# Where the tiles lie in SBUF: rooms laid out in a given order, with gaps of 32 bytes between kinds of tile

## The chip, the cores and the metric

The kernel runs on one core of one Trainium2 chip. The metric is the device time of one execution in microseconds; three runs of the kernel before gave 2304.89 to 2305.59 us, median 2305.21.

## What is computed

Two layers of a decoder trunk over 1024 tokens of width 1024, in float32. Each layer has two head groups side by side (a retention group and a differential attention group), an output projection, and a SwiGLU feed-forward part:

```
def reference(x, attn_norm, w_in, ...):
    h = x
    for l in range(DEPTH):                              # DEPTH = 2
        u = rmsnorm(h, attn_norm[l])
        rq, rk, rv, rg, dq, dk, dv = split(u @ w_in[l])
        ret = silu(rg) * rmsnorm(retention_chunkwise(rq, rk, rv), ret_norm[l])
        dif = rmsnorm(diff_attention(dq, dk, dv, lam), diff_norm[l]) * (1.0 - lam_init)
        h = h + concat([ret, dif]) @ w_out[l]
        u = rmsnorm(h, ffn_norm[l])
        h = h + (silu(u @ w_gate[l]) * (u @ w_up[l])) @ w_down[l]   # hidden size 2816
    return rmsnorm(h, final_norm)
```

## The kernel before

Activations lie feature-major: 128 features on the partitions, tokens along the row. Every large product is made of TensorE matmuls with a 128x128 block of weights as the stationary operand and 512 tokens of an activation as the moving operand. Float32 accuracy comes from splitting each operand into a high part and a low part and adding three matmuls: high weights times high activations, high weights times low activations, low weights times high activations. `mm3` (L270 to L272) does this for the projections, the output projection and the tail of the down projection; `product` (L246 to L248) does it for gate, up and most of the down projection, which go by a Strassen-like scheme of seven products in place of eight. `tm_pair` (L305 to L307) makes token-major values with the roles turned round: the activation `u` is stationary and the weights move, 256 columns at a time.

```
for i, (bh, bl) in enumerate(b):
    c = slice(P * i, P * i + P)
    mm(ps, lhsT=wh[:, c], rhs=bh, ...)       # L246
    mm(ps, lhsT=wh[:, c], rhs=bl, ...)       # L247
    mm(ps, lhsT=wl[:, c], rhs=bh, ...)       # L248
```

Each matmul is an instruction pair: a weight load (LDWEIGHTS, shown as PEld) and the matmul itself (MATMUL, shown as PE). The weight load of the next matmul runs beside the matmul before it.

The names of the tiles are their tags. `w` (12 tiles of 128x512) holds the split weights. The moving operands of the big products are in `u` (4 tiles of 8x512), `ka`, `v` and `sp` (4 tiles of 1024 each); the line `TAGS7 = ["u", "u", "ka", "v", "u", "u", "sp"]` says which tag holds the moving operand of each of the seven products, so four of seven are in `u` and one each in `ka`, `v` and `sp`. Raw weights arrive by DMA in `wr` (some in `kb`), the stream of hidden activations in `mx`; `a4` (shown as `a`) holds the residual stream and attention tiles, `t2` (shown as `t`) is for temporaries, and `acc`, `nx`, `ny`, `z`, `m` are small. PE's order is written out by hand, and in the feed-forward part the order of ScalarE (ACT), VectorE (DVE), GpSimd (POOL) and the DMA queue (SP) too; elsewhere a scheduler orders those four.

A tag gets its room in SBUF (a fixed number of buffers) when it is first asked for, one room behind the other along each partition, in steps of 32 bytes. All big tiles are multiples of 2048 bytes long, and every slice that TensorE reads of the big tiles begins at a multiple of 512 bytes in its tile, so for all the big products the place of an operand modulo 256 is that of its room. The rooms in the built program of before, in bytes modulo 256:

| room | w | u | ka | v | mx | t2 | sp | a4 | wr | kb | acc |
|---|---|---|---|---|---|---|---|---|---|---|---|
| before, modulo 256 | 224 | 224 | 224 | 224 | 224 | 224 | 96 | 96 | 96 | 96 | 96 |
| moving minus `w`, modulo 256 | | 0 | 0 | 0 | | | 128 | | | | |

Of the kernel before, what the change touches and what calls it, by code (L numbers as in the profile page):

```python
# [13 lines left out]
R32 = mybir.dt.float32r  # L14
# [4 lines left out]
P = 128  # L19
D = 1024  # L20
T = 1024
KT = D // P
NH = 2
HT = T // NH
# [5 lines left out]
FAST = 16  # L30
TAILS = [2, 4]
TAGS7 = ["u", "u", "ka", "v", "u", "u", "sp"]
RAWS = ["wr", "wr", "wr", "kb", "kb"]
EPS = 1e-6
NEG = -3.0e38
# [83 lines left out]
class Line:  # L119


    def __init__(self):
        self.n, self.tasks, self.products, self.w, self.made = -1, {}, [], {}, 0
# [23 lines left out]
class Trunk:  # L147
    def __init__(self, tc, ctx, a):
        self.tc, self.nc, self.a = tc, tc.nc, a
        pool = lambda name, **kw: ctx.enter_context(tc.tile_pool(name=name, bufs=1, **kw))  # L150
        self.sb = pool("sb")
        self.ps = pool("ps", space=bass.MemoryType.PSUM)
        self.dr = pool("dr", space=bass.MemoryType.DRAM)
        self.n = 0
        self.wi = 0
        self.consts()


    def t(self, tag, bufs, shape, dt=F32):
# [290 lines left out]
    def seven_second(self, h, gcol, b, keep, line):  # L450
# [10 lines left out]
        b11, b21 = [keep[i // 2][:, c[i % 2]] for i in range(4)], [keep[2 + i // 2][:, c[i % 2]] for i in range(4)]  # L461
        b += [self.views(TAGS7[2]), self.views(TAGS7[3]), None, self.views(TAGS7[5]), None]
        two = [self.big("sp") for _ in range(2)]
# [6 lines left out]
        def sub(out, x, z, q=None, i=0):  # L470
            v(out=out, in0=x, in1=z, op=ALU.subtract)
            if q is not None:
                nc.scalar.copy(b[q][i][0], out)
# [12 lines left out]
        def room(q):  # L486
            b[q] = self.views(TAGS7[q])
        ops += [lambda i=i: sub(b11[i], t22[i], t12[i]) for i in r]
# [561 lines left out]
    def right_factors(self, line, fast, m0):  # L1050
# [14 lines left out]
        def one(q, i):  # L1065
            if not b[q]:
                b[q] += self.views(TAGS7[q])
            self.part(stage[q, i - i % 2][:, 512 * (i % 2):512 * (i % 2) + 512], b[q][i],
# [9 lines left out]
    def down_fast(self, line, h, at, f0, b, m):  # L1078
# [3 lines left out]
        for e in range(2):  # L1082
            self.factors(line, at + 2 * e, {j: n0 + 2 * j + e for j in range(7)}, None,
                         [RAWS[(m + e) % 5], RAWS[(m + 2 + e) % 5]],
                         [n for n in range(n0, n0 + 14) if n % 3 == 0])
# [25 lines left out]
    def layer(self, l, h, us, w_first, norm1, after):  # L1111
# [22 lines left out]
        keep = [self.big("mx") for _ in range(4)]  # L1134
        b = [self.views(tag) for tag in TAGS7[:2]]
        self.two_halves(h, 4, ws, rhs, ["mm"], self.seven_first(h, 16 + 8 * l, b, keep))
# [130 lines left out]
```

## Time and profile before

| what | value |
|---|---|
| median of 3 runs | 2305.21 us (2304.89 to 2305.59) |
| profiled execution, its own time | 2305.69 us |
| its span (first to last instruction) | 2303.9 us |
| granted TensorE clock, mean | 0.995 |
| PE busy | 2262.5 us (98%), 11328 matmuls |
| PEld busy | 1897.3 us (82%), 11328 weight loads |
| DVE, ACT, POOL busy | 1391.0, 1008.9, 762.5 us |
| DMA queue | 28.9% of 16 engines' span |

The profiled execution took 1.8 us more than its span, and is 0.5 us above the median. PE's busy time counts matmuls that are pipelined: a 512-column matmul is shown as some 390 ns long while the next one starts some 230 ns after it, so two stand one over the other and what counts for the time is the distance from start to start. A wait of PE is shown in the columns on idle time and in the list of waits.

### The profile page before, as it was taken

The page shows a single profiled execution, that of the slowest core. Times are in us where ns is not written, and L with a number is a line of the kernel's source. Part 1 is how long each engine was busy: PE and PEld are TensorE (multiplying, and loading weights), DVE is VectorE, ACT ScalarE, POOL GpSimd, SP SyncE. Part 2 cuts the span into 40 slices and gives each one's busy share as a digit, 9 for nine tenths or more (in the row PEclk, how much of TensorE's full clock was granted, in tenths as well). Part 3 has the DMA queues.
Part 4 walks back from the last instruction along what each step waited for, and adds up shares of the span by engine and source line. Part 5 has one row for each costly group of instructions (what it writes and reads, how often), then busy time and mean ns, then how long its engine had stood idle before and what let it go on. Part 6 is the DMA issues. An engine that isn't in the chain of part 4 may idle for free.

```text
span 2303.9 us, 30680 instructions
## 1 busy us (share of the span) xinstructions
PE 2262.5 (98%) x11328; PEld 1897.3 (82%) x11328; DVE 1391.0 (60%) x2576; ACT 1008.9 (44%) x1905; POOL 762.5 (33%) x608
## 2 busy tenths in 40 slices
PE   8999999999999999999999999999999999999998
PEld 5888898887788888888888888988878888888887
DVE  8777603987534333895567775058874434359856
ACT  5666623445333333543257665244443333344332
POOL 3111212122545455336121112211234545544350
PEclk9999999999999999999999999999999999999999
DMA  5212121112332332752232222102123232346422
GB/s 166 75 47 65 46 92 40 53 55 64 123 115 92 114 106 89 232 185 94 73 99 55 56 65 92 55 29 74 55 87 119 89 118 90 110 148 200 157 65 74
DMA packets 74214, 216.58 MB, mean 94 GB/s; under 512 B 8016, under 2 KB 10064, under 8 KB 74064
## 3 DMA queue, kind: packets, MB, share of 16 engines
q1 hardware_dynamic: 74064, 214.62, 28.9%
q8 instruction: 89, 1.46, 0.3%
q14 instruction: 61, 0.50, 0.1%
HBM read 162.16 MB, written 44.04 MB: 90 GB/s over the span
## 4 chain that ended last, share of the span: by engine, by line
PE 82%; DVE 10%; DMA 2%; ACT 2%; issue 2%; POOL 1%; DVEq 0%; SPq 0%; ACTq 0%; POOLq 0%
PE ps_mm L246 7%; PE ps_mm L248 7%; PE ps_mm L247 7%; PE ps_mm L271 7%; PE ps_mm L270 7%; PE ps_mm L272 7%; PE ps_s L247 4%; PE ps_s L246 4%; PE ps_s L248 4%; PE ps_mm L307 3%; PE ps_mm L305 3%; PE ps_mm L306 3%; PE ps_t L246 3%; PE ps_t L248 3%; PE ps_t L247 3%
## 5 line engine op out<-in xcount | busy, mean ns | idle before, releaser
L223 POOL TENSOR_TENSOR w<-wr,w 128x512 fp32r<-128x512 f32 x278 | 390.5, 1418 | 469.4 <-ACT w L222 436.9
L263 POOL TENSOR_TENSOR w<-wr,w 128x512 fp32r<-128x512 f32 x140 | 184.9, 1327 | 577.7 <-ACT w L262 520.5
L270 PE MATMUL ps_mm<-u,w 128*128 128x512 f32 (+1 forms) x735 | 295.9, 403 | 0.0
L271 PE MATMUL ps_mm<-u,w 128*128 128x512 f32 (+1 forms) x735 | 287.1, 391 | 2.0 <-DVE u L432 2.0
L272 PE MATMUL ps_mm<-u,w 128*128 128x512 f32 (+1 forms) x735 | 287.3, 391 | 0.0
L222 ACT CAST w<-wr 128x512 fp32r<-128x512 f32 x312 | 187.8, 619 | 143.7 <-DVE wr L893 88.3
L246 PE MATMUL ps_mm<-u,w 128*128 128x512 f32 x432 | 168.8, 391 | 0.1
L247 PE MATMUL ps_mm<-u,w 128*128 128x512 f32 x432 | 168.4, 390 | 0.0
L248 PE MATMUL ps_mm<-u,w 128*128 128x512 f32 x432 | 168.3, 390 | 0.0
L272 PEld LDWEIGHTS ps_mm<-u,w 128*128 128x128 f32 x735 | 138.0, 188 | 30.2
L271 PEld LDWEIGHTS ps_mm<-u,w 128*128 128x128 f32 x735 | 138.4, 188 | 25.9 <-DVE u L432 2.7
L270 PEld LDWEIGHTS ps_mm<-u,w 128*128 128x128 f32 x735 | 138.3, 188 | 23.8
L942 ACT COPY t<-ps_mm 128x512 f32<-128x512 f32 x76 | 44.6, 586 | 246.3 <-PE ps_mm L248 246.1
L262 ACT CAST w<-wr 128x512 fp32r<-128x512 f32 x140 | 85.7, 619 | 129.1 <-PE ps_mm L271 39.0
L305 PE MATMUL ps_mm<-w,u 128*128 128x256 f32 x448 | 128.6, 287 | 0.0
L307 PE MATMUL ps_mm<-w,u 128*128 128x256 f32 x448 | 127.8, 285 | 0.1
L306 PE MATMUL ps_mm<-w,u 128*128 128x256 f32 x448 | 127.6, 285 | 0.0
L223 POOL TENSOR_TENSOR w<-t,w 128x512 fp32r<-128x512 f32 x52 | 74.7, 1436 | 147.7 <-ACT w L222 147.7
L559 DVE CUSTOM_DVE_ANT_0 sp<-ps_s,wr 128x512 f32<-128x512 f32 (+2 forms) x192 | 102.8, 551 | 33.2 <-PE ps_s L557 32.2
L563 ACT ACTIVATE sp<-sp,m 128x256 f32<-128x256 f32 (+7 forms) x128 | 99.2, 775 | 50.8 <-DVE m L562 50.1
L851 DVE TENSOR_TENSOR a<-a,ps_mm 128x512 f32<-128x512 f32 (+1 forms) x148 | 98.5, 666 | 33.4 <-PE ps_mm L248 19.9
L246 PE MATMUL ps_t<-u,w 128*128 128x512 f32 x288 | 113.2, 393 | 4.8 <-ACT t L942 4.8
(386 smaller groups left out, 5832.7 us busy)
## 6 DMA issues: line engine op xcount, KB each, us to landing
wr<-wts SPq DMA_DIRECT2D x190, 512.0 KB, 3.7
mx<-s_fast SPq DMA_DIRECT2D x56, 512.0 KB, 4.9
s_fast<-mx SPq DMA_DIRECT2D x48, 512.0 KB, 5.0
kb<-ka SPq DMA_DIRECT2D x64, 128.0 KB, 2.3
s_rest<-mx SPq DMA_DIRECT2D x12, 512.0 KB, 2.9
kb<-wts SPq DMA_DIRECT2D x12, 512.0 KB, 6.0
mx<-s_rest SPq DMA_DIRECT2D x12, 512.0 KB, 3.8
a<-xT SPq DMA_DIRECT2D x16, 256.0 KB, 5.4
```

The lines of the kernel that those rows point to most:

```text
L222: nc.scalar.copy(h, src)
L223: (eng or nc.gpsimd).tensor_tensor(out=o, in0=src, in1=h.bitcast(F32), op=ALU.subtract)
L246: mm(ps, lhsT=wh[:, c], rhs=bh, start=first and i == 0, stop=False, skip_group_check=True)
L247: mm(ps, lhsT=wh[:, c], rhs=bl, start=False, stop=False, skip_group_check=True)
L248: mm(ps, lhsT=wl[:, c], rhs=bh, start=False, stop=i == 3, skip_group_check=True)
L263: nc.gpsimd.tensor_tensor(out=o, in0=raw[:, cols], in1=h.bitcast(F32), op=ALU.subtract)
L270: mm(out, lhsT=lh, rhs=rh, start=first, stop=False)
L271: mm(out, lhsT=lh, rhs=rl, start=False, stop=False)
L272: mm(out, lhsT=ll, rhs=rh, start=False, stop=last)
L305: mm(o, lhsT=uh, rhs=wh, start=k == 0, stop=False)
L306: mm(o, lhsT=uh, rhs=wl, start=False, stop=False)
L307: mm(o, lhsT=ul, rhs=wh, start=False, stop=k == KT - 1)
```

## The change

`rooms()` runs ahead of everything else and asks once for one tile of certain tags, in the order of a list; this fixes where their rooms lie. A number in the list puts a gap of that many bytes. The other tags follow by first use, as before. Nothing else differs: on every engine the instructions, their order, their shapes and their waits are the same as before, and only the addresses are others.

```
+ROOMS = ["w", 32, "ka", 32, "v", 32, "sp", "nx", "ny", "u"]
...
+        self.rooms()
         self.consts()
+
+    def rooms(self):
+
+        for i, x in enumerate(ROOMS):
+            if isinstance(x, int):
+                self.const(f"gap_{i}", [P, x // 4])
+            elif x == "u":
+                self.t("u", 4, [P, KT, HT], R32)
+            elif x in ("w", "t2", "acc"):
+                self.t(x, {"w": 12, "t2": 5, "acc": 2}[x], [P, 512])
+            elif x in ("nx", "ny"):
+                self.t(x, 2, [P, 4])
+            elif x in ("z", "m"):
+                self.t(x, 4, [P, 4])
+            else:
+                self.big(x)
```

`nx` and `ny` take 128 bytes between them, so `u` comes 128 behind `sp`. The rooms in the built program of the changed kernel:

| room | w | u | ka | v | mx | t2 | sp | a4 | wr | kb | acc |
|---|---|---|---|---|---|---|---|---|---|---|---|
| after, modulo 256 | 128 | 96 | 160 | 192 | 64 | 64 | 224 | 64 | 64 | 64 | 64 |
| moving minus `w`, modulo 256 | | 224 | 32 | 64 | | | 96 | | | | |

## The prediction

> **What bounds the kernel now.** I read the page's first two parts, then the list of PE's waits, then PE's groups by form, and last the timeline of single matmuls.
>
> ```profile
> span 2303.9 us, 30680 instructions
> ...
> PE 2262.5 (98%) x11328; PEld 1897.3 (82%) x11328; DVE 1391.0 (60%) x2576; ACT 1008.9 (44%) x1905; POOL 762.5 (33%) x608
> ...
> PEclk9999999999999999999999999999999999999999
> ...
> PE 82%; DVE 10%; DMA 2%; ACT 2%; issue 2%; POOL 1%; DVEq 0%; SPq 0%; ACTq 0%; POOLq 0%
> ```
>
> PE is busy in 98% of the span, at nearly full clock in every slice, and 82% of the chain that ended last is PE. The list of PE's waits says the same from the other side; these are its two longest:
>
> ```profile
> PE ps_mm L289 <- DMA a<-xT: 5.2, 1, 5.2
> PE ps_t L246 <- ACT t L942: 4.8, 2, 2.4
> ```
>
> So the time is the sum of the distances from one matmul's start to the next, and the other engines follow. An edit that only moves addresses counts where it changes that distance.
>
> **Does an address change it? The trace of before holds two cases.** The moving tiles `u`, `ka`, `v` lie 0 bytes off the weights `w` modulo 256, `sp` 128 bytes off. The groups by form (busy us, mean ns of one):
>
> ```profile
> L270 PE MATMUL ps_mm<-u,w 128*128 128x512 f32 x729 | 294.3, 404 | 0.0
> L272 PE MATMUL ps_mm<-u,w 128*128 128x512 f32 x729 | 285.6, 392 | 0.0
> L271 PE MATMUL ps_mm<-u,w 128*128 128x512 f32 x729 | 285.4, 392 | 2.0 <-DVE u L432 2.0
> L246 PE MATMUL ps_mm<-u,w 128*128 128x512 f32 x432 | 168.8, 391 | 0.1
> L247 PE MATMUL ps_mm<-u,w 128*128 128x512 f32 x432 | 168.4, 390 | 0.0
> L248 PE MATMUL ps_mm<-u,w 128*128 128x512 f32 x432 | 168.3, 390 | 0.0
> ...
> L247 PE MATMUL ps_t<-u,w 128*128 128x512 f32 x288 | 112.6, 391 | 0.0
> ...
> L247 PE MATMUL ps_s<-u,w 128*128 128x512 f32 x224 | 87.2, 389 | 0.0
> ...
> L246 PE MATMUL ps_mm<-sp,w 128*128 128x512 f32 x216 | 85.7, 397 | 2.8 <-DVE t L954 2.8
> L248 PE MATMUL ps_mm<-sp,w 128*128 128x512 f32 x216 | 85.3, 395 | 0.0
> L247 PE MATMUL ps_mm<-sp,w 128*128 128x512 f32 x216 | 85.1, 394 | 0.0
> ...
> L247 PE MATMUL ps_mm<-ka,w 128*128 128x512 f32 x216 | 84.1, 389 | 0.0
> ...
> L247 PE MATMUL ps_s<-v,w 128*128 128x512 f32 x192 | 74.7, 389 | 0.0
> ```
>
> Same instruction, same shape, same lines: 389 to 391 ns where moving tile and weights lie 0 apart, (397 + 395 + 394) / 3 = 395.3 ns where they lie 128 apart. A shown duration contains the next matmul's start, so I check it on the timeline (start us, length us), where twelve `sp` matmuls are followed by `u`:
>
> ```profile
> 560.65 0.40 PE L246 MATMUL ps_mm<-sp,w 128*128 128x512 f32 x1
> 560.89 0.39 PE L247 MATMUL ps_mm<-sp,w 128*128 128x512 f32 x1
> ...
> 563.44 0.39 PE L246 MATMUL ps_mm<-u,w 128*128 128x512 f32 x1
> 563.68 0.40 PE L247 MATMUL ps_mm<-u,w 128*128 128x512 f32 x1
> 563.91 0.39 PE L248 MATMUL ps_mm<-u,w 128*128 128x512 f32 x1
> 564.14 0.39 PE L246 MATMUL ps_mm<-u,w 128*128 128x512 f32 x1
> ...
> 564.59 0.39 PE L248 MATMUL ps_mm<-u,w 128*128 128x512 f32 x1
> ...
> 566.18 0.39 PE L246 MATMUL ps_t<-u,w 128*128 128x512 f32 x1
> ```
>
> Twelve `sp` matmuls take 563.44 - 560.65 = 2.79 us, 232.5 ns from start to start. The first three `u` matmuls behind them still take 233 ns each (564.14 - 563.44 = 0.70 us); the last seven before 566.18 take 1.59 us, 227 ns each. Two things follow. The difference of 5 ns in the durations is one of start-to-start distance. And at 0 bytes the short distance is a state that PE settles into: for the first matmuls behind a disturbance the same operands cost what 128 bytes cost.
>
> By the Trainium skill none of this should be. The page "TensorE: Matmul & The Clock Gate", section "Step-by-step: what each phase is for", says that loading the next tile's weights takes no SBUF read bandwidth from the running matmul, since the two have ports of their own. By that rule the change is worth nothing and the sum stays at 2305. The rows of `sp` against those of `u` speak against it; its rival is weighed below.
>
> **The change, part by part.** The order, the shapes and the waits of all instructions stay, so each term is a count of matmuls by a change of distance. The new residues are 224 (that is, 32 below) for `u`, 32 for `ka`, 64 for `v`, 96 for `sp`. No row of before shows any of these, so each is bounded by the rows at 0 and at 128 and, below, by the shortest matmul of any of these tiles (minimum / median / maximum ns):
>
> ```profile
> L247 PE MATMUL ps_mm<-u,w x432: 387/389/398, 504.0 to 2210.3; 128*128 128x512 f32 x144
> ...
> L247 PE MATMUL ps_mm<-ka,w x216: 387/389/397, 539.3 to 2199.4; 128*128 128x512 f32 x108
> ...
> L247 PE MATMUL ps_mm<-sp,w x216: 387/393/399, 560.9 to 2221.3; 128*128 128x512 f32 x108
> ```
>
> None of the three goes below 387 ns in any phase, and at 0 bytes the median of 389 is already within 2 ns of it. So there is little to win at `u`, `ka`, `v` (1 to 3 ns each) and 6 ns to lose.
>
> - `u` in gate, up and down (L246 to L248): 3 x (432 + 288 + 224) = 2832 matmuls, now 390 ns. At the price of `sp`: 2832 x 5.3 = +15.0 us; at the median of 389: -2.8.
> - `u` in the projections (L270 to L272): 3 x 729 = 2187, now 392 (L270's 404 holds the waits at a group's start; I price it as the other two). 2187 x 3.3 = +7.2; or 2187 x -3 = -6.6.
> - `ka`: 648 matmuls at 389: 648 x 6.3 = +4.1, or 0. `v`: 576 at 389: +3.6, or 0.
> - `sp`, 648 matmuls, 128 to 96: I take 0, since 128 is the nearest row; -4.1 if it comes down to 389.
>
> Which end for `u` and `ka`? By distance, 32 bytes are nearer to 0 than to 128. I still take the end of 128 for all three, because the timeline shows that the long distance is what PE runs at whenever it is out of the settled state, with 0 bytes too: the long one looks like the general case, the short one like a coincidence of two streams that must meet exactly. It is a choice with little behind it, hence its modest chance. For `v` at 64, halfway, the same choice has more behind it.
>
> - `tm_pair` (weights moving, `u` stationary, 256 columns) goes from 0 to 32. Its rows, and one of 128 bytes:
>
> ```profile
> L305 PE MATMUL ps_mm<-w,u 128*128 128x256 f32 x448 | 128.6, 287 | 0.0
> L306 PE MATMUL ps_mm<-w,u 128*128 128x256 f32 x448 | 127.6, 285 | 0.0
> ...
> L601 PE MATMUL ps_o<-a,v 128*128 128x256 f32 x160 | 40.0, 285 | 0.0
> ```
>
> At 256 columns 0 and 128 bytes cost the same within 2 ns, so I take 0; the ends are 1344 x -2 = -2.7 and 1344 x 5.3 = +7.1.
>
> - ACT and POOL read and write the same rooms. Their rows (POOL's with two inputs) at 128 bytes (`wr` or `kb` with `w`) and at 0 (`t` with `w`, `mx` with `u`):
>
> ```profile
> L223 POOL TENSOR_TENSOR w<-wr,w 128x512 fp32r<-128x512 f32 x278 | 390.5, 1418 | 469.4 <-ACT w L222 436.9 <-issue 15.0 <-PE ps_s L248 8.6
> ...
> L223 POOL TENSOR_TENSOR w<-t,w 128x512 fp32r<-128x512 f32 x52 | 74.7, 1436 | 147.7 <-ACT w L222 147.7
> L223 POOL TENSOR_TENSOR w<-kb,w 128x512 fp32r<-128x512 f32 x28 | 40.9, 1462 | 76.9 <-ACT w L222 76.9
> L238 POOL TENSOR_TENSOR u<-mx,u 128x512 fp32r<-128x512 f32 x14 | 20.4, 1463 | 8.5 <-ACT u L237 7.6 <-PE ps_mm L271 0.4 <-PE ps_mm L272 0.4
> ```
>
> 1418 and 1462 at 128, 1436 and 1463 at 0: no order by address. I take 0. Were there a few per cent, POOL's idle time in the first row (469.4 us beside 390.5 busy) and PE's short waits above cover it. The gap tiles and the first request of each tag issue nothing.
>
> Sum: 15.0 + 7.2 + 4.1 + 3.6 = +29.9 us on the profiled execution's 2305.7 us (span 2303.9 and 1.8 around it): 2335.6; the median of before is 0.5 lower, so 2335. Both ends: all at the low ones gives -2.8 - 6.6 - 4.1 - 2.7 = -16, thus 2289; all high with `tm_pair` gives +37, thus 2342, and a residue worse than 128 would go beyond.
>
> **Rivals.**
> 1. Nothing happens (2305). Either the two ports never meet, and `sp` is slow for another reason (it ends each set of seven products, and its users wait on DVE's sums), or the settled state is wide enough to take 32 and 64 bytes. For it: medians of 389 at three different tiles, and the distance argument. Against: twelve `sp` matmuls in a row at 232.5 ns with no wait between them. It decides if `u` keeps a median of 389.
> 2. Faster (2293). PE settles at 224 as at 0, or sooner behind each disturbance, and `sp` at 96 comes into reach: -4.1 for `sp`, -6.6 for the projections' `u`, -2.8 for the other `u`, less what `ka` and `v` may give back; I take -12. The place is L270 to L272: 392 ns against 389 is what the way into the settled state costs today. It decides if `sp` falls under 391 while `u` does not rise.
> 3. Only the tiles 64 and more off lose (2309): `v` +3.6, `tm_pair` a little, `u` and `ka` unchanged.
>
> A further sentence of the skill points at more: the same page's "Back-to-back issue gap" gives N / 2.4 + 2.5 ns, thus an estimate of 216 ns at 512 columns, 11 ns under the settled 227. By that page some 6200 matmuls would gain up to 68 us if addresses alone stood between. The minimum of 387, at 0 and at 128 alike, shows no such matmul.
>
> **How the numbers follow.** Forecast (`u` at the price of 128, with most or all of the others): 0.46. Rival 1: 0.21. Rival 2: 0.25. Rival 3: 0.08, half of it within 0.2%. Changes of 0.2% (4.6 us) are about what a measurement of this kernel can tell from none. So faster 0.25, same 0.25, slower 0.50. The range of 8 in 10 must reach both sides: down to 2291, which leaves out only the best of rival 2, and up to 2345, a little over the high ends. Within the forecast alone it is 2322 to 2347, since `u` may be dearer or cheaper at 224 than `sp` at 128.
>
> **What would show it.** In the changed kernel's groups by form, `u` of L246 to L248 at 394 to 397 shows the forecast right, 389 to 390 shows it wrong, whatever the others do. `ka`, `v` and `sp` are three more readings of the same curve, at 32, 64 and 96. L305 to L307 outside 283 to 289 would upset the zero for `tm_pair`. PE's idle time should stay as small as it is; if it grows, or if POOL's 1418 moves by more than 50 ns, another engine feels the addresses and the argument from PE alone fails. What would make it wrong is mainly the choice of the end for 224: 5019 of the 6243 matmuls priced hang on that one residue.

## Result: 1.1% slower, and the profile after

The changed kernel takes 2330.22 us (median of 4 runs, 2329.69 to 2331.28) beside 2305.1 us for the kernel before on the same chip: a ratio of 1.0108 (95% interval 1.0093 to 1.0123). The profiled execution took 2329.69 us, its span 2327.9 us, at the same granted clock of 0.995. In the changed kernel's file the numbers of the lines are 18 higher: the product is L264 to L266, the projections L288 to L290, `tm_pair` L323 to L325.

The page of the changed kernel, its busy times and the shares of the chain that ended last:

```profile
span 2327.9 us, 30680 instructions
...
PE 2291.4 (98%) x11328; PEld 1895.1 (81%) x11328; DVE 1386.7 (60%) x2576; ACT 1010.4 (43%) x1905; POOL 758.4 (33%) x608
...
PE 86%; DVE 9%; ACT 2%; issue 1%; DMA 0%; POOL 0%; DVEq 0%; ACTq 0%; POOLq 0%
```

PE alone is busier, by 2291.4 - 2262.5 = 28.9 us; ACT, DVE, POOL and the weight loads stay within 4.5 us. PE's idle time (span less busy) went from 41.4 to 36.5 us, so 4.9 of the 28.9 us did not reach the end. The list of PE's waits has the same two at its top as before:

```profile
PE ps_mm L307 <- DMA a<-xT: 5.5, 1, 5.5
PE ps_t L264 <- ACT t L960: 4.7, 2, 2.4
```

The groups by form (busy us, mean ns of one) show where the 28.9 us are:

```profile
L288 PE MATMUL ps_mm<-u,w 128*128 128x512 f32 x729 | 296.9, 407 | 0.0
L289 PE MATMUL ps_mm<-u,w 128*128 128x512 f32 x729 | 288.2, 395 | 1.8 <-DVE u L450 1.8
L290 PE MATMUL ps_mm<-u,w 128*128 128x512 f32 x729 | 287.6, 395 | 0.0
L266 PE MATMUL ps_mm<-u,w 128*128 128x512 f32 x432 | 171.1, 396 | 0.0
...
L323 PE MATMUL ps_mm<-w,u 128*128 128x256 f32 x448 | 127.2, 284 | 0.0
L324 PE MATMUL ps_mm<-w,u 128*128 128x256 f32 x448 | 126.2, 282 | 0.2 <-POOL w L281 0.2
L325 PE MATMUL ps_mm<-w,u 128*128 128x256 f32 x448 | 126.0, 281 | 0.0
...
L265 PE MATMUL ps_t<-u,w 128*128 128x512 f32 x288 | 115.3, 400 | 0.0
...
L265 PE MATMUL ps_s<-u,w 128*128 128x512 f32 x224 | 88.6, 396 | 0.0
...
L266 PE MATMUL ps_mm<-sp,w 128*128 128x512 f32 x216 | 85.2, 394 | 0.0
L265 PE MATMUL ps_mm<-ka,w 128*128 128x512 f32 x216 | 85.1, 394 | 0.0
L266 PE MATMUL ps_s<-v,w 128*128 128x512 f32 x192 | 75.6, 394 | 0.0
L265 PE MATMUL ps_s<-v,w 128*128 128x512 f32 x192 | 75.3, 392 | 0.0
L264 PE MATMUL ps_s<-v,w 128*128 128x512 f32 x192 | 74.9, 390 | 0.0
```

The reader is to see that every group with `u`, `ka` or `v` moving grew, most by 3 to 7 ns per matmul, `v` by 1 to 5 (the 400 of `ps_t` holds a stretch at half speed that is shown further below), `sp` hardly at all, and `tm_pair`, with 256 columns and the roles turned round, became 3 to 4 ns cheaper. The timeline shows that it is again the distance from start to start, as in the quoted stretch of before:

```profile
564.92 0.39 PE L264 MATMUL ps_mm<-u,w 128*128 128x512 f32 x1
...
567.01 0.40 PE L264 MATMUL ps_mm<-u,w 128*128 128x512 f32 x1
```

Nine `u` matmuls in 2.09 us, 232 ns each, where the last seven of before took 227 ns each. Further on in such rows `u` goes on at 231.7 and 234.8 ns in turn: the settled state that it had at 0 bytes is gone.

### The profile page after: what moved, and what is told of

Same layout as the page of the kernel before. It is cut to its first block, busy times and chain, and to the rows that moved or that the text cites. A ratio compares the mean times of both kernels' runs of the same rounds, so it can differ in the third digit from the quotient of the medians.

```text
span 2327.9 us, 30680 instructions
## 1 busy us (share of the span) xinstructions
PE 2291.4 (98%) x11328; PEld 1895.1 (81%) x11328; DVE 1386.7 (60%) x2576; ACT 1010.4 (43%) x1905; POOL 758.4 (33%) x608
## 4 chain that ended last, share of the span: by engine, by line
PE 86%; DVE 9%; ACT 2%; issue 1%; DMA 0%; POOL 0%; DVEq 0%; ACTq 0%; POOLq 0%
PE ps_mm L264 8%; PE ps_mm L265 8%; PE ps_mm L266 8%; PE ps_mm L289 7%; PE ps_mm L288 7%; PE ps_mm L290 7%; PE ps_s L266 4%; PE ps_s L265 4%; PE ps_s L264 4%; PE ps_t L264 3%; PE ps_t L265 3%; PE ps_t L266 3%; PE ps_mm L325 2%; PE ps_mm L323 2%; PE ps_mm L324 2%; PE ps_s L574 1%
## 5 line engine op out<-in xcount | busy, mean ns | idle before, releaser
L288 PE MATMUL ps_mm<-u,w 128*128 128x512 f32 (+1 forms) x735 | 298.6, 406 | 0.0
L290 PE MATMUL ps_mm<-u,w 128*128 128x512 f32 (+1 forms) x735 | 289.3, 394 | 0.0
L266 PE MATMUL ps_mm<-u,w 128*128 128x512 f32 x432 | 171.1, 396 | 0.0
L265 PE MATMUL ps_mm<-u,w 128*128 128x512 f32 x432 | 170.9, 396 | 0.0
L264 PE MATMUL ps_mm<-u,w 128*128 128x512 f32 x432 | 170.9, 396 | 0.0
L290 PEld LDWEIGHTS ps_mm<-u,w 128*128 128x128 f32 x735 | 138.1, 188 | 32.9
L288 PEld LDWEIGHTS ps_mm<-u,w 128*128 128x128 f32 x735 | 138.3, 188 | 25.8
L323 PE MATMUL ps_mm<-w,u 128*128 128x256 f32 x448 | 127.2, 284 | 0.0
L325 PE MATMUL ps_mm<-w,u 128*128 128x256 f32 x448 | 126.0, 281 | 0.0
L264 PE MATMUL ps_t<-u,w 128*128 128x512 f32 x288 | 115.4, 401 | 4.7 <-ACT t L960 4.7
```

The lines of the kernel that those rows point to most:

```text
L264: mm(ps, lhsT=wh[:, c], rhs=bh, start=first and i == 0, stop=False, skip_group_check=True)
L265: mm(ps, lhsT=wh[:, c], rhs=bl, start=False, stop=False, skip_group_check=True)
L266: mm(ps, lhsT=wl[:, c], rhs=bh, start=False, stop=i == 3, skip_group_check=True)
L288: mm(out, lhsT=lh, rhs=rh, start=first, stop=False)
L290: mm(out, lhsT=ll, rhs=rh, start=False, stop=last)
L323: mm(o, lhsT=uh, rhs=wh, start=k == 0, stop=False)
```

## The experiments

All start from the changed kernel and alter the list ROOMS (three of them also give one tag two rooms), so one row of residues (moving tile less weights, modulo 256) describes each. The theory: what a matmul of 512 columns costs hangs on where its moving tile lies against the weights modulo 256, whatever the tile, the line or the place in the program. The rivals are named with the runs.

**All tiles at 0.** `sp` too goes to the weights' residue.

```
-ROOMS = ["w", 32, "ka", 32, "v", 32, "sp", "nx", "ny", "u"]
+ROOMS = ["w", "ka", "v", "sp", "u", "mx", "t2", "a4", "wr", "kb", "acc"]
```

> All big rooms (w, ka, v, sp, u, mx, t2, a4, wr, kb, acc) lie at one residue modulo 256, so every moving tile is 0 bytes off its weights. Theory 1 (what counts is moving minus weights, modulo 256, and 0 is the cheap one): sp falls from 395 to 389-390 ns (648 x 6 = -3.9 us), the mixed pairs of before (u with kb, ka with a, some 400 matmuls) fall by about 5 (-2 us), u, ka, v stay at 389-391; time about 2299. Theory 2 (sp is slow since it ends each set of seven products and its users wait): sp stays at 395, time 2305. Theory 3 (a tile's own place modulo 256 counts, whatever the weights' place): all tiles have moved to another residue than before, so u, ka and v move away from 389 as well.

Measured: 2299.61 us, ratio to before 0.9972 (0.9961 to 0.9983). Groups by form:

```profile
L266 PE MATMUL ps_mm<-u,w 128*128 128x512 f32 x432 | 168.1, 389 | 0.0
...
L323 PE MATMUL ps_mm<-w,u 128*128 128x256 f32 x448 | 128.1, 286 | 0.0
...
L265 PE MATMUL ps_mm<-sp,w 128*128 128x512 f32 x216 | 84.1, 389 | 0.0
```

`sp` falls from 394 to 389 ns, the value of all others. So `sp` was dear for its address and not for its place in the program. From start to start, against weights in `w` and with distances over 300 ns left out, the mean falls by 5.8 ns for `sp` (4.5 us over its 770 matmuls) and by 0.3 ns for `u` (1.6 us over its 5138), though `u` lies at 0 in both; the reason for the second is in the section on why the prediction was right. Against the few weights that lie in `kb`, 128 off in before, the same `u` falls from 232.8 to 226.7 ns.

**The residues crossed over:** `sp` at 0 (256 modulo 512), and `u`, `ka`, `v` at 128.

```
+ROOMS = ["w", "z", "u", "ka", "v", "mx", "t2", "nx", "ny", "sp", "a4", "wr", "kb", "acc"]
```

> The rooms of w alone are put 128 bytes further against all other rooms of before: u, ka, v become 128 off w, sp becomes 0 off (256 modulo 512); the other rooms keep their distances among one another. Theory 1: a cross-over, u, ka, v go to 394-396 and sp falls to 389-390; 2832 x 5.3 + 2187 x 3.3 + 4.1 + 3.6 - 4.1 = +26, about 2331. Theory 2: sp stays at 395 and u at 390, 2305. Theory 3: only w changed its relation, so moving tiles keep their order (sp slower than u). If the period were 512 and not 256, sp would not fall to 389 although u rises.

Measured: 2328.52 us, ratio 1.0101 (1.0086 to 1.0116).

```profile
L266 PE MATMUL ps_mm<-u,w 128*128 128x512 f32 x432 | 170.6, 395 | 0.0
...
L266 PE MATMUL ps_mm<-ka,w 128*128 128x512 f32 x216 | 85.3, 395 | 0.0
...
L265 PE MATMUL ps_mm<-sp,w 128*128 128x512 f32 x216 | 84.3, 390 | 0.0
...
L266 PE MATMUL ps_s<-v,w 128*128 128x512 f32 x192 | 75.8, 395 | 0.0
```

The tiles change prices: what was 389 is 395, and `sp` at 256 bytes costs 390. The price follows the address, and it repeats with 256 bytes.

**`u` alone moved, to 224; the rest as before.**

```
+ROOMS = ["w", "ka", "v", "mx", "t2", "z", "sp", "a4", "wr", "kb", "acc", "nx", 32, "u"]
```

> Only u is put where the change puts it (224 off w); ka, v, mx, t2 stay 0 off and sp, a, wr, kb, acc 128 off as before. Theory 1: u at 395-396, ka and v 389, sp 395; tm_pair (w minus u is 32) 281-284 as in the changed kernel. 2832 x 5.5 + 2187 x 3.3 - 1344 x 3 = +19, about 2324, most of the change's +25. Theory 3b (the small rooms or the neighbours' order matter, not u's distance): 2305.

Measured: 2323.0 us, ratio 1.0075 (1.006 to 1.009), thus +17 us of the change's +25.

```profile
L265 PE MATMUL ps_mm<-u,w 128*128 128x512 f32 x432 | 170.9, 396 | 0.0
...
L324 PE MATMUL ps_mm<-w,u 128*128 128x256 f32 x448 | 125.9, 281 | 0.0
...
L264 PE MATMUL ps_mm<-ka,w 128*128 128x512 f32 x216 | 84.7, 392 | 0.0
...
L266 PE MATMUL ps_mm<-ka,w 128*128 128x512 f32 x216 | 84.0, 389 | 0.0
...
L266 PE MATMUL ps_s<-v,w 128*128 128x512 f32 x192 | 74.7, 389 | 0.0
```

The tile that moved changed, and with it `tm_pair`, which has the same `u` as its stationary operand. `ka` at 0 is 3 ns dearer in its first two lines, since it now follows a `u` at another residue.

**`u` left at 0, the others moved** (`ka` 32, `v` 64, `sp` 96).

```
+ROOMS = ["w", "u", "mx", "t2", 32, "ka", 32, "v", 32, "sp", 32, "a4", "wr", "kb", "acc"]
```

> The other half of the change: ka 32, v 64, sp 96 off w, u back at 0. Theory 1: u 389-391, ka 395, v 390-394, sp 394-398 as in the changed kernel, tm_pair back at 285-287: 648 x 6 + 576 x 3 + 648 x 1 = +6, about 2311. e3 and e4 together should add up to the change's +25. If they do not, the parts act on one another.

Measured: 2313.0 us, ratio 1.0033 (1.002 to 1.0045), thus +7 us. The two halves add up: 17 + 7 = 24 beside 25 for the whole.

```profile
L266 PE MATMUL ps_mm<-u,w 128*128 128x512 f32 x432 | 168.1, 389 | 0.0
...
L324 PE MATMUL ps_mm<-w,u 128*128 128x256 f32 x448 | 127.6, 285 | 0.0
...
L266 PE MATMUL ps_mm<-ka,w 128*128 128x512 f32 x216 | 85.4, 396 | 0.0
```

**Other residues for each tile:** `u` 64, `v` 160, `sp` 192, `ka` 224.

```
+ROOMS = ["w", "mx", "t2", "nx", "u", "ny", "a4", "wr", "kb", "acc", 32, "v", 32, "sp", 32, "ka"]
```

> The same kinds of distance, given to other tiles: u 64 off w, ka 224, v 160, sp 192. Theory 1 (the distance sets the price, whichever tile it is): u takes what v had at 64 in the changed kernel (L264 390, L265 392, L266 394, in place of 389-390 at 0), ka takes what u had at 224 (395-396), and v and sp give two new readings at 160 and 192, expected with the long ones at 394-397; 5019 x 3 + 648 x 6 + 576 x 6 + 0 = +22, about 2327. Theory 3 (the tile's place in the chain of products sets it): v stays at 390-394, u at 395-396, 2330. 64 would then be the only distance besides 0 that is partly cheap.

Measured: 2314.53 us, ratio 1.0038 (1.0024 to 1.0052). The time expected was 2327: a miss by 12 us.

```profile
L290 PE MATMUL ps_mm<-u,w 128*128 128x512 f32 x729 | 286.8, 393 | 0.0
L266 PE MATMUL ps_mm<-u,w 128*128 128x512 f32 x432 | 170.4, 394 | 0.0
...
L264 PE MATMUL ps_mm<-u,w 128*128 128x512 f32 x432 | 169.4, 392 | 0.0
L323 PE MATMUL ps_mm<-w,u 128*128 128x256 f32 x448 | 126.1, 281 | 0.0
...
L324 PE MATMUL ps_mm<-w,u 128*128 128x256 f32 x448 | 125.0, 279 | 0.0
...
L265 PE MATMUL ps_mm<-sp,w 128*128 128x512 f32 x216 | 85.2, 395 | 0.0
```

Two reasons: `u` at 64 costs 392 to 394 ns and in the projections only 1 ns more than before, and `tm_pair`, whose weights now lie 192 from `u`, takes 279 to 281 ns in place of 285 to 287, some 8 us over 1344 matmuls. The expectation had priced the second at nothing.

**Whose weights: the matmul's own, or those loaded beside it?** The high and the low part of the weights get rooms of their own. In the control both lie at 0:

```
-        h, o = self.t("w", 12, [P, 512], R32), self.t("w", 12, [P, 512], R32)
+        h, o = self.t("wh", 6, [P, 512], R32), self.t("wl", 6, [P, 512], R32)
...
+ROOMS = ["wh", "wl", "ka", "v", "sp", "u", "mx", "t2", "a4", "wr", "kb", "acc"]
```

> Control for the next run: all rooms at one residue as in e1, but the high and the low weights in rooms of their own (6 tiles each, handed out in the same turn). Every theory: as e1, about 2300, with 389-391 ns in L264, L265 and L266 alike.

Measured: 2299.2 us, ratio 0.9974 (0.9963 to 0.9986), like all tiles at 0. Splitting the room alone does nothing. Then the low part 128 off:

```
+ROOMS = ["wh", "ka", "v", "sp", "u", "mx", "t2", "a4", "wr", "kb", "acc", "z", "wl"]
```

> As e6, but the room of the low weights lies 128 bytes off everything else; high weights and moving tiles stay at one residue. L264 runs on high weights while the next matmul's high weights load, L265 on high weights while the low ones load, L266 on low weights while the next high ones load. Theory A (a matmul is held by the weight load beside it, that of the next matmul): L265 is long (394-397), L264 and L266 short or in between while PE finds its state again. Theory B (a matmul is held by the place of its own weights): L266 is long, L264 and L265 short. Theory C (only the moving tile's own place): all as in e6. Time by A or B: one third of the 6243 matmuls by 5 ns and more, +10 to +25, 2310 to 2325.

Measured: 2319.13 us (2 runs), ratio 1.0061 (1.0041 to 1.0081).

```profile
L266 PE MATMUL ps_mm<-u,wl 128*128 128x512 f32 x432 | 171.5, 397 | 0.0
L265 PE MATMUL ps_mm<-u,wh 128*128 128x512 f32 x432 | 171.1, 396 | 0.0
L264 PE MATMUL ps_mm<-u,wh 128*128 128x512 f32 x432 | 168.5, 390 | 0.0
```

From start to start L264 takes 226.7 ns, L265 232.5 and L266 234.1. The moving tiles lie as in the control, so their own place alone explains nothing here. L265 has its own weights at 0, but beside it the load of L266's low weights runs, 128 off: it is dear. So the place of the next weights, loaded beside a running matmul, counts; the matmul's own weights alone don't explain it. L266, with its own weights 128 off and L264's load at 0 beside it, is dear too, which the load beside it alone doesn't explain either. It may be its own weights, or something carried over from L265. Against a carry-over speaks that L264, right behind L266, is short at once, and that in the next experiment a matmul at 0 between two at 128 stays short; but no run separates the two. The weight load beside L266 is shown longer as well, 192 ns where the two others take 188. Only L264, where both are at 0, keeps 390. By what path the place of the weights acts stays open.

**One part of the moving operand 128 off.** `ka` gets two rooms, `kh` at 0 and `kl` 128 off, handed out in pairs. In the built program it is the high part that lies in `kl` (L270 and L272 of this kernel) and the low part in `kh` (L271), the reverse of what the expectation says.

```
+        if tag == "ka":
+            self.kc += 1
+            return self.t("kh" if self.kc % 4 in (1, 2) else "kl", 2, [P, 1024], dt)
...
+ROOMS = ["w", "kh", "v", "sp", "u", "mx", "t2", "a4", "wr", "kb", "acc", "z", "kl"]
```

> All weights and all other rooms at one residue as in e1, but of the moving tile ka the low half (kl) lies 128 bytes off, the high half (kh) 0 off. In each triple of the third product the middle matmul alone (low moving half, L270) has a distance of 128; the third one (L271, high moving half) has its own and its companion's weights and its moving tile all at one residue. Theory A with carry-over (one matmul at an expensive distance disturbs PE, and the next one pays as well): L270 and L271 are both long, about 396, L269 is 389, as the three lines in e7. Theory A without carry-over (in e7 the third line was long because of its own low weights): only L270 is long, L271 at 389-390. Time: 432 or 216 matmuls by 6 ns on e1, +1 to +3 us, so about 2302.

Measured: 2302.66 us, ratio 0.9987 (0.9977 to 0.9997).

```profile
L270 PE MATMUL ps_mm<-kl,w 128*128 128x512 f32 x216 | 84.9, 393 | 0.0
L272 PE MATMUL ps_mm<-kl,w 128*128 128x512 f32 x216 | 84.5, 391 | 0.0
...
L271 PE MATMUL ps_mm<-kh,w 128*128 128x512 f32 x216 | 84.2, 390 | 0.0
```

The matmul at 0 between two at 128 stays short, and the two at 128 cost 2 to 4 ns more, not 6. The size isn't explained: a residue in a long row costs more than the same residue in two of every three matmuls. `v`, which lies at 0 and comes next behind this `ka`, is dearer too: 393, 392 and 390 ns in its three lines, where the run with all tiles at 0 has 389.

**`mx` at 192.** `mx` moves with `u` stationary in 192 matmuls of 256 columns; the permuted run suggested that 192 is cheap there.

```
+ROOMS = ["w", "ka", "v", "sp", "u", "t2", "a4", "wr", "kb", "acc", "nx", "z", "mx"]
```

> As e1, but mx lies 192 off. In e5 the 256-column matmuls of tm_pair, whose weights move and whose stationary tile is u, were shortest with weights minus u at 192 (279-281 in place of 284-287). mx holds half of the first value weights of each layer, some 180 such matmuls: theory 1 says they go from 291-295 to about 286 at most, -1 us, and some 150 matmuls that use mx as stationary weights or hold other halves lose as much: 2299, the same as e1 within what can be told. If all 256-column matmuls came down, distance would not be the reason.

Measured: 2298.41 us, ratio 0.9971 (0.996 to 0.9982).

The mean of the first of the three lines stays at 294 ns, as in the repeat of all tiles at 0 below. But that mean is raised by a few matmuls: 17 of the 192 distances here and 14 there are over 152 ns, most of them waits or matmuls near 35 us, where the granted clock is lower (0.50 from 33 to 38 us here). Minimum, median and maximum of the durations show the rest, here:

```profile
L323 PE MATMUL ps_mm<-mx,u x64: 276/277/415, 29.9 to 1202.4; 128*128 128x256 f32 x64
```

and in the repeat of all tiles at 0:

```profile
L323 PE MATMUL ps_mm<-mx,u x64: 277/283/416, 30.7 to 1204.0; 128*128 128x256 f32 x64
```

The median falls from 283 to 277, and the distance from start to start, without those few, from 119.5 to 115.4 ns. So the cheapness of 192 carries over to these matmuls, as theory 1 had it. It is worth 175 x 4.1 ns = 0.7 us, too little to show in the time, and the mean that was to fall to 286 is not the figure that shows it.

**All tiles at 0 once more, over five rounds.** The list is that of the first experiment.

> e1 once more in five rounds, beside e9: theory 1 says 0.997 of before again, sp at 389-391.

Measured: 2299.07 us (10 runs), ratio 0.9974 (0.9965 to 0.9984). With the first experiment this is the version that beats both kernels: 0.26% under before, 31 us under the change. The run with `mx` at 192 is not told apart from it.

**The curve.** Mean distance from the start of one 512-column matmul to the next, from the start times of all consecutive matmuls of a trace, by the moving tile less the weights that the next matmul loads, modulo 256; distances over 258 ns (waits, starts of groups) are left out, for 256 columns those over 152 ns. In these runs the matmul's own weights and the next ones lie in the same room. The row of 256 columns is `tm_pair` (moving weights less stationary `u`), and `mx` against `u` at 224.

| residue | 0 | 32 | 64 | 96 | 128 | 160 | 192 | 224 |
|---|---|---|---|---|---|---|---|---|
| 512 columns, ns | 227.4 | 233.4 | 229.8 | 234.2 | 232.9 | 233.5 | 233.0 | 233.2 |
| matmuls behind it | 7793 | 786 | 4962 | 786 | 6864 | 817 | 984 | 4981 |
| 256 columns, ns | 119.7 | 116.8 | | | 118.8 | | 114.2 | 118.1 |

The columns come from different runs of those above: 0 from all tiles at 0, 128 from the residues crossed over, 32 and 96 from `u` left at 0, 64, 160 and 192 from the permuted run, 224 from `u` alone moved (256 columns: 32 from `u` alone moved, 224 from the changed kernel). The runs agree where they overlap: before gives 227.7 at 0 and 232.6 at 128, after gives 233.2 at 224, 232.9 at 32, 229.9 at 64 and 234.1 at 96.

## Why the prediction was right, point by point

Forecast 2335 from +29.9 us; measured 2330.22, and in the profiled spans +24.0. Busy time, from the groups of both kernels:

| term | forecast, us | measured, us |
|---|---|---|
| `u`, L246 to L248 | +15.0 | +19.3 |
| `u`, projections | +7.2 | +7.4 |
| `ka` | +4.1 | +3.6 |
| `v` | +3.6 | +1.7 |
| `sp` | 0 | +0.9 |
| `tm_pair` | 0 | -4.6 |
| all other groups (the rest of PE's +28.9) | 0 | +0.6 |
| PE's idle time | 0 | -4.9 |
| span | +29.9 | +24.0 |

That the sum came within 6 us is partly luck: `u` in L246 to L248 was priced 4.3 us too low, and `v`, `tm_pair` and the idle time together 11.4 us too high.

- **The end of 128 for 224** held: 396 ns was what L264 to L266 needed to show, and 233.2 ns from start to start at 224 stands beside 232.9 at 128. The run with `u` alone moved shows it alone. No row of before had 224 and the prediction had little behind the choice, so that it was the right end is in part luck. Some 1.7 us of the 19.3 are not the addresses: near 1700 us eight `u` matmuls of the changed kernel stand 427 ns apart, at a granted clock of 0.50 from 1700.0 to 1703.4 us, and before has no such stretch there. It comes behind a wait of PE for ACT's `t`, 2.35 us long; before has the same wait at 1685 us, 2.41 us long, with no such stretch behind it.

```profile
1700.62 0.63 PE L266 MATMUL ps_t<-u,w 128*128 128x512 f32 x1
1701.05 0.63 PE L264 MATMUL ps_t<-u,w 128*128 128x512 f32 x1
```

- **The reason given for that choice** was that the long distance is the general case and 0 a coincidence. The curve bears this out but for 64: five of the seven other residues lie within 0.6 ns of each other and a sixth, 96, a little above them.
- **The settled state** is real, but what ends it was read too widely. Over the 67 places in before where `u` follows `sp`, the first `u` matmuls take 231, 233.5 and 230 ns and from the fourth on 226.8; in the run with all tiles at 0 (its repeat) the same places take 226.8, 226.5 and 226.7 from the first. An ordinary change of tile disturbs nothing: the disturbance was the other residue of `sp`. (In the same run, behind a stretch at half speed that ends near 553 us, `u` is long at 0 as well: 231, 236, 228, 232 and 231 ns.) The residue of the tile ahead accounts for some 1.0 of `u`'s 1.6 us in the first experiment (67 places at 15 ns) and for `ka`'s 392 with `u` alone moved. The prediction had seen it at one place and had counted 1 to 3 ns to win at `u`, without saying that moving `sp` would win them.
- **`v` at 64** was the mis-sized term: +1.7, not +3.6. The rows of `v` by line, 390, 392, 394, stand for a cycle: behind the first matmul of each row, which mostly takes 237 or 238 ns, they take 226, 229 and 232 ns from start to start in turn, again and again. "Halfway between two rows" was no argument for the price of either.
- **`tm_pair`** was put at 0 with a lower end of -2.7, and two of its three rows, 281 and 282, fall below the 283 to 289 allowed. Two equal rows (0 and 128) did not bound a curve that dips between them: 119.7 at 0, 116.8 at 32 and 114.2 at 192 in the other runs.
- **POOL and ACT at 0**: POOL's first group is within the 50 ns named.

```profile
L241 POOL TENSOR_TENSOR w<-wr,w 128x512 fp32r<-128x512 f32 x278 | 386.4, 1403 | 484.1 <-ACT w L240 457.4 <-issue 18.4 <-PE ps_s L266 8.3
```

- **Idle time** fell by 4.9 us instead of staying. It is the largest part of the 6 us between forecast and span. That longer matmuls use up PE's short waits is the likely reason, but it was not tested; one such wait, for DVE's `t` ahead of `sp`, went from 2.8 to 0.9 us.

Rival 1 fell with the first two experiments: `sp` was slow for its address. That the two ports never meet is not borne out either, since the place of the next weights changes the running matmul's time, though no run shows where the two meet. Rival 2 fell with `u` at 396; what it hoped for, `sp` coming down to 389, needs 0 and not 96. Rival 3 fell too, since 32 and 224 cost as much as 128 and only 64 is cheap: distance from 0 is no measure.

Rival 1 had the support of the Trainium skill, "TensorE: Matmul & The Clock Gate", section "Step-by-step: what each phase is for", by which loading the next weights takes no read bandwidth from a running matmul. As a rule for the time these runs disagree: L265 in the run with the low weights 128 off took 396 ns beside that load and 389 beside one at 0. The same page's "Back-to-back issue gap" gives N / 2.4 + 2.5 ns as the gap of an isolated matmul, an estimate of 216 ns at 512 columns, and a measured spacing of some 131 ns for a stream of weight loads and matmuls of that length. The shortest mean of any residue here is 227.4, so even at 0 this form reaches neither.

## What to carry to other kernels

Where a long row of matmuls is the bound and the same two kinds of tile are its operands throughout, look at their addresses modulo 256: here equal residues for weights and moving tiles were the best of eight, 6 ns of 227 a matmul, 1.3% between the worst and best layout of one and the same program. A group that is a few ns slower than its neighbours of the same shape is worth a row of the address map before its waits are blamed, and one tile at another residue also slows the next few matmuls of its neighbours. Measure the curve for each shape: 256 columns had another order than 512.

## What the runs showed of the hardware that was not expected

- The curve is not monotonic: 64 bytes off costs 2.4 ns more than 0, 32 and 96 cost 6 and 6.8 (table above).
- The extra time comes in short cycles. At 128, `sp` of before alternates between 229 and 237 ns from start to start; at 64, `v` goes through 226, 229 and 232.
- Behind a matmul stream at another residue, a stream at 0 needs 3 to 8 matmuls until it runs at 227 ns: in the crossed-over run, `sp` (0) behind `u` (128) takes 231.7, 232.6, 230.8, 227.0 and then 226.7. `ka` behind `u` takes 5 in the run with `u` alone moved, `v` behind the split `ka` takes 8.
- With 256 columns, 192 bytes is the best of the five residues measured, 114.2 ns beside 119.7 at 0 for `w` against `u`, and 115.4 beside 119.5 for `mx` against `u`.
- The place of the weights loaded beside a matmul matters: 396 ns where they alone are 128 off, 390 where neither they nor its own are. With its own 128 off and the others at 0 it takes 397, which may be its own weights or a carry-over. By what path isn't settled.
